# A hybrid decoder block in f32: how much fill each attention step is given

## The chip, the cores and the metric

The kernel runs on one core of a Trainium2 chip. The metric is device time in microseconds (us) of one execution, as the median of several. A core has five engines that run side by side and wait for each other through semaphores: TensorE (PE, matmuls; PEld its weight loads), VectorE (DVE), ScalarE (ACT), GpSimd (POOL) and SyncE (SP, which issues most DMAs). [...]

## The reference

One layer, 1024 tokens behind 16 meta tokens, model width 1024:

```python
h = rmsnorm(x, norm_g)
proj = jnp.einsum('bld,dn->bln', h, w_in)
u_pool, z_pool, q, k, v, z_attn, f_logit, g_pool, g_attn = jnp.split(proj, _split_points(), axis=-1)
y_pool = causal_multiscale_pool(u_pool, pool_w, pool_scale) * jax.nn.silu(z_pool)
log_f = jax.nn.log_sigmoid((f_logit + b_forget).astype(jnp.float32))
y_attn = forgetting_attention(q, k, v, log_f).reshape(B, L, ATTN_WIDTH) * jax.nn.silu(z_attn)
merged = (jax.nn.sigmoid(g_pool) * jnp.einsum('blc,cd->bld', y_pool, w_up_pool)
          + jax.nn.sigmoid(g_attn) * jnp.einsum('blc,cd->bld', y_attn, w_up_attn))
return x + jnp.einsum('bld,de->ble', merged, w_out)
```

The attention has 8 heads of width 64. The logit of query t and key s is q.k/8 plus the sum of the log forget gates between s and t, masked to be causal; then softmax and the product with v. A final rmsnorm follows and the meta tokens are dropped.

## The kernel before

**Precision.** Each f32 operand is split into a high part and a remainder, and a product is made of three matmuls (high x high, high x low, low x high), or two for the attention's score and value products, which carry both parts in one operand. The splits are work of ACT, DVE and POOL.

**Stages.** First the normalised input is transposed and q, k and v of the first pair of heads are projected. Then comes the attention, to about 460 us of the span. Then the gate projections (L973), the two up-projections (L170) and the output projection (L1232).

**The attention** works on 16 units: 4 pairs of heads, 2 heads of a pair, 2 halves of 512 queries. Keys come in blocks of 128 (`KB`). A unit of the first half has five key blocks, one of the second half nine. On the causal edge blocks get narrower: the widths are 512, 400, 272, 144, 16 for the first half, and four times 512 ahead of the same five for the second; these last five touch the diagonal.

- A *score step* (`qk`) makes two matmuls into a PSUM bank `ps` (L678, L679; two such banks), adds the gate term and, on the diagonal, the mask while copying the scores out (L685 DVE, L687 ACT), and updates a running maximum (L690 for the first block, L692 for the others).
- `maxes` finishes the maximum over the keys: two transposes, a reduction and two small maxima on DVE with small ACT copies between them, up to L710, which writes the maximum for all partitions.
- A *softmax step* (`soft`) subtracts the maximum (L719 DVE), takes the exponential (L720 ACT), splits the result in a high part (L723 ACT) and a remainder (L724 DVE), adds the block to the row sums (L730, L732 POOL), and makes the value product of the block two before it (`av`, L740: two matmuls into `po`). The remainder and high part have three buffers each (`NPH`), `LAG` is 2. The value products of a unit's last two blocks follow after all its steps.
- `finish` reads `po` out and stores it and the row sums.

In the loop over the units (L799 on) turn i lays the score steps of unit i+1 among the softmax steps of unit i (`merged`): both lists are spread evenly by width. So an even turn has the scores of a nine-block unit among the softmax of a five-block unit, and an odd one the other way round.

**The fill.** Between the steps PE is given other matmuls, the *fill*: the projections of q, k and v for the next pair of heads (with due times) and, freely, the projections of the pooling input and of the two gates (`f_u`, `f_raw`), which are evacuated by ACT and spilled to DRAM by SP. `Fill.pull(ns)` takes fill, matmul by matmul, until its booked price `mm_ns` (0.4219 ns a column, at least 107 ns) has used up ns; what was overdrawn is carried on as debt. What is left when the units are through is run by `F.drain()`. Who gets how much is written out in four places:

- each step of `merged` gets max(0, `PACE` x (DVE's time by a formula) - (PE's own time in the step)); the formulas stand in `a_steps` (scores) and `c_steps` (softmax);
- each of a unit's last two value products gets `LATENCY` ahead of it;
- `maxes` gets `LM1` = 1400 and `LM2` = 3200 (the first unit 2200 more);
- the gate computation ahead of the units gets ten times `LATENCY` in three pulls.

**The order.** PE's instructions run in the order of the program, which is written out by hand. Those of the other engines, in the attention, are ordered by the compiler's scheduler from their dependencies, priorities and its own expectation of when they can start. Once ordered, each engine takes its instructions strictly in that order. `after(x, y)` puts x behind y on their engine; `put` orders a transfer behind the last spill issued before it, `stores[-1]`.

In turn 13 the first weights of the gate stage are loaded (`g_raw0`), and in turn 14 ACT splits them (L821).

Of the kernel before, what the change touches and what calls it, by code (L numbers as in the profile page):

```python
# [22 lines left out]
KB = 128  # L23
# [7 lines left out]
PADS = {"lead": 32, "rest": 0}  # L31
HALVES = ((0, 512), (512, 1024))
PJ, PT = 3, 2
PACE = 1.67
LATENCY = 1800.0
LAT2 = 1600.0
LM1, LM2 = 1400.0, 3200.0
FIRST = 2200.0
NPH = 3
LAG = 2  # L40
# [5 lines left out]
def r32(ap):  # L46
    return ap.bitcast(F32)


def mm_ns(n):  # L50
    return max(n * 0.4219, 107.0)
# [3 lines left out]
def tile_hybrid_block(ctx, tc, x, meta, norm_g, w_in, b_forget, pool_w, pool_scale,  # L55
# [56 lines left out]
    def after(ins, prev):  # L112
        tc.add_manual_dep(ins.ins, prev.ins.name,
                          mybir.DependencyInfo(mybir.DependencyClass.NoSync, mybir.DependencyReason.DATA),
                          reason="order")
# [284 lines left out]
    F = Fill()  # L400
# [181 lines left out]
    def rows_of(t):  # L582
        return t.rearrange("(k p) c -> p k c", p=128)

    def put(dst, src):
        after(nc.sync.dma_start(dst, src), stores[-1])
# [56 lines left out]
    class Unit:  # L643
# [9 lines left out]
        def a_steps(self):  # L653
            for b in range(self.nb):
                w = 512 - self.c0[b]
                yield w, 1.04 * w + 70, 2 * mm_ns(w), (lambda b=b: self.qk(b))

        def c_steps(self):
            for b in range(self.nb):
                w = 512 - self.c0[b]  # L660
                yield w, 1.75 * w + 130, 2 * mm_ns(w), (lambda b=b: self.soft(b))

        def qk(self, b):
            p, e, q0, t0, kb, c0 = self.p, self.e, self.q0, self.t0, self.kb[b], self.c0[b]
# [95 lines left out]
    def merged(a, c):  # L760
        out_ = []
        for lst in (a, c):
            tot = sum(s[0] for s in lst) or 1
            acc = 0.0
            for s in lst:
                out_.append(((acc + 0.5 * s[0]) / tot, s))
                acc += s[0]
        for _, (w, dve, pe, f) in sorted(out_, key=lambda t: t[0]):
            f()
            F.pull(max(0.0, PACE * dve - pe))  # L770

# [8 lines left out]
    def pair_fill(p):  # L780
        if p < 4:
            F.add(f"q{p}", f_q(p))
            F.add(f"k{p}", f_k(p))
            F.add(f"v{p}", f_v(p), 4 * p - 2)
            F.add(f"v{p}", v_blocks(p, (6, 9), (0, 1)), 4 * p - 2, apart=True)
# [4 lines left out]
    def sums_at(i, tr):  # L790
        trs.append(tr)
        sums_of(i)
        if i % 4 == 1 and i > 1:
            add_y(i // 4 - 1)

    units = [Unit(p, e, half) for p in range(4) for e in range(2) for half in range(2)]
    merged(list(units[0].a_steps()), [])
    units[0].maxes(FIRST)
    for i, u in enumerate(units):  # L799
        nxt = units[i + 1] if i + 1 < 16 else None  # L800
        F.now = i
        if nxt is not None and nxt.p != u.p:
            F.until(f"q{nxt.p}", f"k{nxt.p}")
        merged(list(nxt.a_steps()) if nxt else [], list(u.c_steps()))
        for b in range(u.nb - LAG, u.nb):
            F.pull(LATENCY)
            u.av(b)
        if i == 1:
            after(nc.scalar.activation(pwh, pw, AF.Copy), exps[-1])
            nc.gpsimd.tensor_tensor(pwl, pw, r32(pwh), op=ALU.subtract)  # L810
        if nxt is not None:
            nxt.maxes(hook=lambda tr: sums_at(i, tr))
        u.finish()
        if i == 13:
            g_raw0 = [gp.tile([128, 2, 512], F32, name="graw", tag="g") for _ in range(2)]
            for k in range(2):
                put(g_raw0[k], rows_of(GSRC[0])[:, 2 * k:2 * k + 2])
        if i == 14:
            g_w0 = [[gp.tile([128, 2, 512], F32R, name="gw0", tag="g") for _ in range(2)] for _ in range(2)]
            for k in range(2):  # L820
                after(nc.scalar.activation(g_w0[0][k], g_raw0[k], AF.Copy), exps[-1])  # L821
                for c in range(0, 2):
                    for h0 in (0, 256):
                        after(nc.gpsimd.tensor_tensor(g_w0[1][k][:, c, h0:h0 + 256], g_raw0[k][:, c, h0:h0 + 256],
                                                      r32(g_w0[0][k][:, c, h0:h0 + 256]), op=ALU.subtract), accs[-1])
        if nxt is not None and nxt.p != u.p:
            F.until(f"v{nxt.p}")
            pair_fill(nxt.p + 1)
# [523 lines left out]
```

## Time and profile before

| | us |
|---|---|
| median of 3 runs | 727.25 (726.98 to 727.72) |
| the profiled execution's own time | 727.18 |
| its span, first to last instruction | 725.5 |

The profile is one execution. Its page gives the busy time of each engine; the view of stages gives the same for stretches of the span; the timeline has a row for each run of equal instructions: start, length, engine, line, operation, tiles, shape, count, and in brackets the idle time of the engine before it and what ended that. The end of a matmul is modelled and lies beyond the start of the next one in a back-to-back stream, so the time a matmul takes in a stream is read from start to start.

### The profile page before, as it was taken

How to read it: one execution, taken by the hardware profiler on the slowest of the kernel's cores; microseconds unless marked ns; L12 is line 12 of the kernel's file. 1: busy time of each engine (PE TensorE's matmuls, PEld its weight loads, DVE VectorE, ACT ScalarE, POOL GpSimd, SP SyncE). 2: the span in 40 equal slices, each digit the busy share in tenths (PEclk: the TensorE clock that was granted, in tenths of full speed). 3: DMA queues.
4: the chain of work that ended last, by engine and by line, in shares of the span. 5: the costliest groups of instructions: out<-in, count | busy, mean ns of one | idle time of the engine just before them, and what ended most of it. 6: DMA issues, size and time to landing. Idle time of an engine off the chain costs nothing.

```text
span 725.5 us, 10804 instructions
## 1 busy us (share of the span) xinstructions
PE 712.8 (98%) x3637; PEld 613.8 (85%) x3637; DVE 506.9 (70%) x913; ACT 422.4 (58%) x930; POOL 330.8 (46%) x409
## 2 busy tenths in 40 slices
PE   8999999999999999999999999999999999999996
PEld 6997999998888898898888878888888888888885
DVE  5753577667688676886768658765877545888775
ACT  6652577557686677676765576252776423525445
POOL 5412236639446584463653666493843010006152
PEclk9999999999999999999999999999999999999998
DMA  9201124782984868838576599486906267761006
GB/s 307 63 26 34 29 84 166 175 262 60 295 201 95 222 173 221 218 90 222 104 202 148 156 265 248 126 301 202 293 12 238 93 219 248 248 245 59 0 2 232
DMA packets 88506, 119.40 MB, mean 165 GB/s; under 512 B 11297, under 2 KB 54305, under 8 KB 86450
## 3 DMA queue, kind: packets, MB, share of 16 engines
q1 hardware_dynamic: 84896, 99.83, 43.0%
q0 software_dynamic: 2256, 16.25, 12.4%
q10 hardware_dynamic: 1298, 2.63, 1.0%
q8 instruction: 28, 0.46, 0.3%
q14 instruction: 28, 0.23, 0.1%
HBM read 92.81 MB, written 53.67 MB: 202 GB/s over the span
## 4 chain that ended last, share of the span: by engine, by line
PE 84%; ACT 3%; DVE 2%; DMA 1%; POOL 1%; issue 1%; POOLq 0%; ACTq 0%; DVEq 0%
PE pj L170 53%; PE pj L1232 8%; PE pj L973 8%; PE po L740 5%; PE pt L973 3%; PE pt L1232 2%; PE ps L679 2%; PE ps L678 2%; PE pj L515 1%; DMA graw<-in_w_in_dram 1%; POOL acc L732 1%; ACT S L687 1%; DMA raw<-in_w_in_dram 1%; ACT S L720 1%; PE pj L300 0%
## 5 line engine op out<-in xcount | busy, mean ns | idle before, releaser
L170 PE MATMUL pj<-hh,whi 128*128 128x512 f32 (+3 forms) x640 | 144.9, 352 | 0.0
L170 PE MATMUL pj<-hh,wlo 128*128 128x512 f32 (+3 forms) x640 | 143.2, 350 | 0.3 <-POOL wlo L434 0.3
L170 PE MATMUL pj<-hl,whi 128*128 128x512 f32 (+3 forms) x640 | 141.9, 350 | 0.0
L158 POOL TENSOR_TENSOR wlo<-raw,whi 128x256 fp32r<-128x256 f32 x116 | 90.7, 826 | 84.4 <-ACT whi L156 33.1
L170 PEld LDWEIGHTS pj<-hh,whi 128*128 128x128 f32 x640 | 108.0, 188 | 12.1 <-ACT hh L223 0.5
L170 PEld LDWEIGHTS pj<-hl,whi 128*128 128x128 f32 x640 | 108.1, 188 | 12.0
L170 PEld LDWEIGHTS pj<-hh,wlo 128*128 128x128 f32 x640 | 108.0, 188 | 12.0 <-POOL wlo L434 0.5
L724 DVE TENSOR_TENSOR pl<-S,ph 128x512 fp32r<-128x512 f32 (+4 forms) x112 | 83.5, 756 | 26.6 <-ACT ph L723 25.7
L732 POOL TENSOR_TENSOR acc<-acc,S 128x272 f32<-128x272 f32 (+4 forms) x80 | 74.4, 930 | 14.5 <-ACT S L720 9.3
L692 DVE TENSOR_TENSOR pt<-pt,S 128x400 f32<-128x400 f32 (+2 forms) x96 | 46.8, 487 | 44.7 <-ACT S L687 43.1
L687 ACT ACTIVATE S<-ps,negc 128x400 f32<-128x400 f32 (+2 forms) x96 | 48.5, 514 | 37.0 <-DVE S L685 33.0
L136 POOL TENSOR_TENSOR gw<-graw,gw 128x256 fp32r<-128x256 f32 x40 | 45.5, 1173 | 29.8 <-ACT gw L953 12.2
L723 ACT ACTIVATE ph<-S 128x512 fp32r<-128x512 f32 (+4 forms) x112 | 52.7, 479 | 9.6 <-PE po L740 9.2
L720 ACT ACTIVATE S<-S 128x512 f32<-128x512 f32 (+4 forms) x112 | 49.8, 478 | 13.3 <-DVE S L719 13.2
L719 DVE TENSOR_TENSOR S<-S,pt 128x512 f32<-128x512 f32 (+4 forms) x112 | 50.7, 498 | 0.6
L1125 DVE TENSOR_TENSOR rl<-pj,rl 128x512 f32<-128x512 f32 x32 | 22.0, 690 | 28.7 <-PE pj L170 28.4
L973 PE MATMUL pj<-gh,gw 128*128 128x512 f32 x180 | 42.0, 389 | 0.0
L156 ACT ACTIVATE whi<-raw 128x512 fp32r<-128x512 f32 x58 | 33.8, 622 | 11.6 <-DMA raw<-in_w_in_dram 5.1
L973 PEld LDWEIGHTS pj<-gh,gw 128*128 128x128 f32 x180 | 33.8, 188 | 7.1
L678 PE MATMUL ps<-qa,ka 128*128 128x512 f32 (+4 forms) x112 | 36.5, 326 | 3.2 <-ACT S L687 3.2
L679 PE MATMUL ps<-ql,ka 128*128 128x512 f32 (+4 forms) x112 | 37.5, 335 | 0.0
L740 PE MATMUL po<-pl,V 128*128 128x512 f32 (+4 forms) x112 | 37.4, 334 | 0.0
(229 smaller groups left out, 1304.7 us busy)
## 6 DMA issues: line engine op xcount, KB each, us to landing
raw<-in_w_in_dram SPq DMA_DIRECT2D x31, 512.0 KB, 5.2
gs<-in_w_in_dram SPq DMA_DIRECT2D x5, 1024.0 KB, 9.9
td<-in_w_out_dram SPq DMA_DIRECT2D x5, 1024.0 KB, 8.4
xt<-in_x_dram SPq DMA_DIRECT2D x8, 512.0 KB, 7.4
sp_gp<-st SPq DMA_DIRECT2D x16, 256.0 KB, 4.6
gs<-gs POOLq DMA_DIRECT2D x4, 1024.0 KB, 9.1
td<-td POOLq DMA_DIRECT2D x4, 1024.0 KB, 11.3
sp_ga<-st SPq DMA_DIRECT2D x16, 256.0 KB, 4.4
```

The lines of the kernel that those rows point to most:

```text
L158: ins = nc.gpsimd.tensor_tensor(lo[:, k:k + 2], raw[:, k:k + 2], r32(hi[:, k:k + 2]), op=ALU.subtract)
L170: nc.tensor.matmul(ps, a, b, start=(i == 0), stop=(i == len(seq) - 1))
L678: nc.tensor.matmul(ps[:kb, c0:], ka[:, k0:k0 + kb], qa[:, q0 + c0:q0 + 512], start=True, stop=False)
L679: nc.tensor.matmul(ps[:kb, c0:], ka[:, k0:k0 + kb], ql[:, q0 + c0:q0 + 512], start=False, stop=True)
L687: nc.scalar.activation(s[:kb, f0:], ps[:kb, f0:], AF.Identity, bias=nb_)
L720: exps.append(nc.scalar.activation(s[:kb, c0:], s[:kb, c0:], AF.Exp))
L723: nc.scalar.activation(ph[:kb, c0:], s[:kb, c0:], AF.Copy)
L724: dves.append(nc.vector.tensor_tensor(pl[:kb, c0:], s[:kb, c0:], r32(ph[:kb, c0:]), op=ALU.subtract))
L732: accs.append(nc.gpsimd.tensor_tensor(acc[:kb, c0:], acc[:kb, c0:], s[:kb, c0:], op=ALU.add))
L740: nc.tensor.matmul(self.po[:, c0:], v, r[:kb, c0:], start=(b == 0 and i == 0), stop=(b == self.nb - 1 and i == 1))
L973: nc.tensor.matmul(ps, op_w[n][p][k // 2][:, k % 2, i * 128:(i + 1) * 128], op_h[n][q][k // 2][:, k % 2], start=start and m == 0, stop=m = ...
L1232: nc.tensor.matmul(ps, pick(A_, k, p)[:, i * 128:(i + 1) * 128], pick(B_, k, q)[:, c0:c1], start=start and n == 0, stop=n == 11, skip_grou ...
```

## The change

Five numbers in the planner's formulas change, and a new constant is used ahead of a unit's last two value products. `LATENCY` itself and its use in the gate computation stay.

```diff
-PACE = 1.67
+PACE = 1.1
 LATENCY = 1800.0
 LAT2 = 1600.0
 LM1, LM2 = 1400.0, 3200.0
+TAIL = 900.0
...
         def a_steps(self):
             for b in range(self.nb):
                 w = 512 - self.c0[b]
-                yield w, 1.04 * w + 70, 2 * mm_ns(w), (lambda b=b: self.qk(b))
+                yield w, 1.05 * w + 165 + 300 * (b * KB + KB > self.t0), 2 * mm_ns(w), (lambda b=b: self.qk(b))
...
         def c_steps(self):
             for b in range(self.nb):
                 w = 512 - self.c0[b]
-                yield w, 1.75 * w + 130, 2 * mm_ns(w), (lambda b=b: self.soft(b))
+                yield w, 2.6 * w + 376, 2 * mm_ns(w), (lambda b=b: self.soft(b))
...
         for b in range(u.nb - LAG, u.nb):
-            F.pull(LATENCY)
+            F.pull(TAIL)
             u.av(b)
```

The added 300 stands for a block that touches the diagonal. No instruction, transfer or buffer is added or taken away: the same fill matmuls stand at other places between the same steps.

## The prediction

> **What bounds the kernel now.** I read the head of the page first.
>
> ```profile
> span 725.5 us, 10804 instructions
> PE 712.8 (98%) x3637; PEld 613.8 (85%) x3637; DVE 506.9 (70%) x913; ACT 422.4 (58%) x930; POOL 330.8 (46%) x409
> ```
>
> TensorE (PE) is busy 98% of the span, VectorE (DVE) 70%. The view of stages shows whether the attention, where the change acts, differs from the stages behind it (columns: length, busy time and count of PE, weight loads, DVE, ACT, POOL, granted clock).
>
> ```profile
> 375.43:398.24 22.81, 22.81 (x108) 19.04 (x107) 16.61 (x32) 14.96 (x35) 10.36 (x15) 1.00 0.71 184
> ...
> 421.36:444.50 23.14, 21.84 (x103) 17.94 (x102) 14.75 (x32) 15.02 (x33) 12.85 (x18) 1.00 0.94 267
> ...
> 555.36:642.40 87.04, 87.04 (x385) 72.10 (x385) 56.02 (x82) 36.99 (x50) 5.76 (x8) 1.00 0.66 226
> ```
>
> The first row is one interval of the attention (one turn of the unit loop): PE is never idle, DVE is busy 73% of it. The second, the last with scores in it, has 1.3 us of idle PE. The third is a stage without any stall. From the chain of work that ended last:
>
> ```profile
> 460.61 12.82 PE pj L170 x56
> ...
> 555.36 87.04 PE pj L170 x384
> ```
>
> In the stall-free stage a 512-column matmul takes 87.04/384 = 0.227 us; the planner books 0.4219 x 512 = 216 ns, so planned fill costs 1.05 times its booked price. The first row is fill that was still left when the last value product was done (12.8 us, run by `F.drain`). Waits of PE in the attention:
>
> ```profile
> PE ps L678 <- ACT S L687: 3.2, 6, 1.3
> ```
>
> All six are one kind: a score matmul waits until ScalarE (ACT) has copied an older score out of one of the two `ps` banks. No value product waits for DVE. The modelled end of a matmul lies after the next one's start, so a stall is longer than its idle time. The timeline of PE gives it from starts:
>
> ```profile
> 84.61 0.66 PE L170 MATMUL pj<-hh,whi 128*128 128x272 f32 x4
> 85.43 0.39 PE L678 MATMUL ps<-qa,ka 128*128 128x272 f32 x1 [0.15 <-ACT S L687]
> ...
> 85.79 0.67 PE L170 MATMUL pj<-hl,whi 128*128 128x272 f32 x4
> 86.69 0.34 PE L678 MATMUL ps<-qa,ka 128*128 128x144 f32 x1 [0.23 <-ACT S L687]
> ...
> 145.79 0.70 PE L170 MATMUL pj<-hh,whi 128*128 128x384 f32 x3
> 147.17 0.50 PE L678 MATMUL ps<-qa,ka 128*128 128x512 f32 x1 [0.69 <-ACT S L687]
> ...
> 200.15 0.63 PE L170 MATMUL pj<-hh,whi 128*128 128x512 f32 x2
> 201.33 0.33 PE L678 MATMUL ps<-qa,ka 128*128 128x144 f32 x1 [0.55 <-ACT S L687]
> ...
> 332.70 0.63 PE L170 MATMUL pj<-hh,wlo 128*128 128x512 f32 x2
> 333.63 0.50 PE L678 MATMUL ps<-qa,ka 128*128 128x512 f32 x1 [0.30 <-ACT S L687]
> ...
> 427.06 1.07 PE L170 MATMUL pj<-hh,whi 128*128 128x512 f32 x4
> 429.42 0.51 PE L678 MATMUL ps<-qa,ka 128*128 128x512 f32 x1 [1.29 <-ACT S L687]
> ```
>
> Start to start, less the run between at 0.227 us a matmul (by width 0.170 for 384 columns and 0.120 for 272), the stalls are 0.34 + 0.42, 0.87, 0.73, 0.48 and 1.45: **4.3 us in all**, 0.6% of the run. The rest of the attention is PE work of fixed length. Fill that is moved does not shorten it: the change can win at most these 4.3 us, and loses by making new stalls.
>
> **The change, part by part.** *What the planner gives out.* A score step of width w got max(0, 1.67(1.04w+70) - 2mm), and gets 1.1(1.05w+165) - 2mm, with 300 more inside the bracket for a block on the diagonal. For 512 columns: 574 to 341 ns, on the diagonal 671. For 400, 272, 144 and 16 columns (always diagonal): 474 to 636, 360 to 596, 153 to 464, 0 to 316. Softmax steps: 1281 to 1446, 1049 to 1220, 783 to 962, 424 to 611, 50 to 245. The two tails: 3600 to 1800 a unit. Summed with the unchanged 4600 of `maxes`: an interval that lays the scores of a nine-block unit among the softmax of a five-block one goes from 15644 to 14931 ns; one with a nine-block softmax from 18473 to 19351; the first scores alone from 1561 to 2683; the last unit from 12312 to 12068. Over 16 units: 268.3 to 269.7 us. So 1.4 us less fill is left for the end, about 11.4 of the 12.8: PE does not run dry, and the stages behind start at the same amount of PE work. No instruction, transfer or wait is added; only PE's order changes, and with it when ACT, DVE, POOL and SP get their evacuations, weight splits and spills.
>
> *More at softmax steps: worth nothing.* The tightest value product that I found:
>
> ```profile
> 225.79 0.75 DVE L724 TENSOR_TENSOR pl<-S,ph 128x272 fp32r<-128x272 f32 x1
> ...
> 226.60 0.37 PE L740 MATMUL po<-ph,V 128*128 128x272 f32 x1
> 226.81 0.29 PE L740 MATMUL po<-pl,V 128*128 128x272 f32 x1
> ```
>
> DVE was done at 226.54, PE came at 226.81: 0.27 us of slack, and no wait. More fill widens that; there was nothing to win. DVE was not late for softmax anywhere.
>
> *Less at the tails, and less at full-width score steps.* Both bring PE sooner to the waits for score copies. Take the last score of a five-block unit (16 columns), the end of its maximum (L710, from which the next softmax starts), and the first and fourth score matmul of the nine-block unit that follows:
>
> ```profile
> 328.51 0.40 PE L678 MATMUL ps<-qa,ka 128*128 128x512 f32 x1
> ...
> 365.78 0.17 PE L678 MATMUL ps<-qa,ka 128*128 128x16 f32 x1
> ...
> 375.43 0.40 PE L678 MATMUL ps<-qa,ka 128*128 128x512 f32 x1
> ...
> 380.06 0.39 PE L678 MATMUL ps<-qa,ka 128*128 128x512 f32 x1
> ...
> 411.74 0.17 PE L678 MATMUL ps<-qa,ka 128*128 128x16 f32 x1
> ```
> ```profile
> 325.79 0.73 DVE L710 STREAM_TRANSPOSE pt<-mz 128x512 f32<-128x512 f32 x1
> ...
> 370.76 0.73 DVE L710 STREAM_TRANSPOSE pt<-mz 128x512 f32<-128x512 f32 x1
> ...
> 416.24 0.73 DVE L710 STREAM_TRANSPOSE pt<-mz 128x512 f32<-128x512 f32 x1
> ```
>
> Last score to next unit's first: 9.65 us on PE. Booked in between: 0+50+3600+4600 = 8250 before, 316+245+1800+4600 = 6961 after, so 1289 x 1.05 = 1.35 less: 8.30. The maximum ends 5.71 (371.49 - 365.78) or, where DVE was prompt, 5.23 us (416.97 - 411.74) after that last score. The longer steps ahead of it let DVE catch up, so I take 5.2 to 5.5. PE then reaches the first score 2.8 to 3.1 us after the maximum, where it was 375.43 - 371.49 = 3.94. First to fourth score: 4.63 before; four steps in between change by -233+165-233-233 = -534 ns, so 4.07. The fourth score comes 6.9 to 7.2 us after the maximum; before it came 8.57.
>
> Its bank is free when ACT has copied the second score. ACT runs the softmax exponentials first (L720, from 372.24 on), then weight splits and copies:
>
> ```profile
> 331.87 1.14 ACT L156 ACTIVATE whi<-raw 128x512 fp32r<-128x512 f32 x2
> 332.91 1.25 ACT L687 ACTIVATE S<-ps,negc 128x512 f32<-128x512 f32 x2
> ...
> 372.24 0.63 ACT L720 ACTIVATE S<-S 128x512 f32<-128x512 f32 x1 [0.92 <-DVE S L719]
> ...
> 375.59 1.14 ACT L156 ACTIVATE whi<-raw 128x512 fp32r<-128x512 f32 x2
> 376.63 0.67 ACT L687 ACTIVATE S<-ps,negc 128x512 f32<-128x512 f32 x1
> 377.33 0.60 ACT L690 ACTIVATE pt<-S 128x512 f32<-128x512 f32 x1
> 377.87 0.58 ACT L342 ACTIVATE st<-pj 128x512 f32<-128x512 f32 x1
> 378.66 0.69 ACT L687 ACTIVATE S<-ps,negc 128x512 f32<-128x512 f32 x1 [0.20 <-PE ps L679]
> ```
>
> In the second group ACT waited only 0.20 us, so without PE the copy could end at 379.15, 7.66 us after the maximum. In the first it released PE at 333.63, 7.11 after 326.52 (and PE, at 328.51 only 1.99 us behind that maximum, stalled). So ACT needs 7.1 to 7.7 us and PE will allow 6.9 to 7.2: a stall of 0 to 0.8 us, middle 0.4, in each of the seven intervals of this kind behind the first. **2.8 us (0 to 5.6)**. Before, three of these seven stalled behind the full-width scores and one at a 144-column score (0.87, 0.48, 1.45, 0.73: 3.5).
>
> *More at narrow score steps.* In front of 85.43 PE gets 97+162 = 259 ns more (x1.05 = 0.27 of the 0.34), in front of 86.69 another 236 (0.25 of 0.42). The copies there are ordered by ACT's queue; I book a gain of 0.4 of the 0.76. The stall at 201.33 sits behind two score steps that together get 585 ns more, and goes.
>
> *The last interval.* Its stall has a cause of its own:
>
> ```profile
> 427.73 1.06 ACT L821 ACTIVATE gw<-graw 128x1024 fp32r<-128x1024 f32 x1 [2.52 <-DMA graw<-in_w_in_dram]
> ```
>
> A score copy lies behind this on ACT. The transfer is issued behind a spill (`put` comes after `stores[-1]`). At that point 2.4 us more fill is done than before (1122 + 7 x (878 - 713) ns, times 1.05), so the spill and the transfer can come up to 2.4 us earlier against PE's scores. I leave 0.5 us of it beyond the ordinary stall, bounds 0 and 1.5.
>
> Sum after: 0.3 (first unit) + 2.8 + 0.5 + 0.3 for stalls like that at 201.33 at new places (bounds 0 and 1, one seen in 15 intervals) = 3.9, against 4.3. The profiled execution took 727.18 us (its span 725.5), 0.07 under the median 727.25; **forecast 727.18 - 0.4 = 726.8**: no change that can be told.
>
> [...]
>
> **The rivals.** *Slower: the score run meets ACT's softmax burst.* Same mechanism as above at its bad end. ACT keeps its order, with weight splits ahead of the second copy (7.7 us), and PE allows 6.9: 7 x 0.8 = 5.6, the last transfer as before (1.5), first unit 0.3, others 1.0: 8.4, or 4.1 more: **731.3**. It decides from a mean stall of 0.6 us a long-score interval on (7 x 0.6 + 0.3 + 0.5 + 0.6 = 5.6, 1.3 over now). For it: two intervals with a lead near 2 us stall today (147.17, 333.63). Against: leads will be 2.8 to 3.1. Chance 0.25.
>
> *Faster: the copies move up.* Only PE's order is written out; the compiler orders ACT by when it expects things ready. If, with scores due sooner, it puts their copies between the exponentials, the second ends under 6.9 us and the seven stalls go: 0.3 + 0.3 + 0.3 left, 3.4 won: **723.8**. For it: exponentials have slack. Against: nothing shows the compiler's view. Chance 0.25.
>
> *The edit does nothing:* total fill differs by 0.5%, softmax was not late, and the stalls are set by ACT's queue wherever PE stands. Then only the first unit's 0.4 goes: 726.8, inside the forecast; its chance is in it.
>
> [...] Chance 0.02, as the stall-free row speaks against it.
>
> **How the numbers follow.** About 0.2% (1.45 us) is what a measurement of this kernel tells from no change. Forecast (within 1.45) 0.48, slower 0.25, faster 0.25 + 0.02. The range takes in most of both rivals: 724.2 to 730.6.
>
> **What would show it.** Right: PE waits remain `ps L678 <- ACT S L687`, now small ones at third and fourth scores of many nine-block units rather than a few large; none at 201 or for L740; the final run of fill near 11.4 us; first score about 3 us behind L710. Wrong: leads under 2.5 us or over 4, waits of L740 for DVE, ACT copying scores between exponentials, or a stall over 1 us at a new place.

## The result, and the profile after

| | us | ratio to before (95%) |
|---|---|---|
| before, 4 runs | 727.12 (726.64 to 727.72) | |
| after, 4 runs | 733.65 (732.87 to 734.59) | 1.009 [1.0073, 1.0107] |
| the profiled execution of after | 732.87, its span 731.2 | |

The change makes the kernel 6.5 us slower; the forecast was 726.8, the range 724.2 to 730.6. From profile to profile the span grew by 731.2 - 725.5 = 5.7 us, and those are what the trace can explain. Lines 38 and up of before are one higher in after (L687 is L688, L821 is L822).

The head of the page of after:

```profile
span 731.2 us, 10818 instructions
PE 713.9 (98%) x3637; PEld 615.6 (84%) x3637; DVE 509.7 (70%) x913; ACT 424.2 (58%) x930; POOL 334.2 (46%) x409
```

PE's count is the same and its busy time 1.1 us more. The waits of PE in the attention (total, times, longest):

```profile
PE ps L679 <- ACT S L688: 7.4, 5, 5.2
...
PE pj L171 <- DVE V L311: 0.8, 1, 0.8
```

The kind is the one of before, but one of the five waits is 5.2 us long. PE's timeline, around it and at the other waits:

```profile
147.47 0.50 PE L679 MATMUL ps<-qa,ka 128*128 128x512 f32 x1 [0.99 <-ACT S L688]
...
241.22 0.50 PE L679 MATMUL ps<-qa,ka 128*128 128x512 f32 x1 [0.70 <-ACT S L688]
...
262.56 0.70 PE L171 MATMUL pj<-hh,whi 128*128 128x512 f32 x2 [0.79 <-DVE V L311]
...
335.60 0.50 PE L679 MATMUL ps<-qa,ka 128*128 128x512 f32 x1 [0.33 <-ACT S L688]
...
424.24 0.39 PE L679 MATMUL ps<-qa,ka 128*128 128x512 f32 x1
...
427.72 0.63 PE L171 MATMUL pj<-hh,whi 128*128 128x512 f32 x2
433.53 0.79 PE L679 MATMUL ps<-qa,ka 128*128 128x512 f32 x1 [5.18 <-ACT S L688]
434.12 0.63 PE L680 MATMUL ps<-ql,ka 128*128 128x512 f32 x1
434.55 1.48 PE L171 MATMUL pj<-hh,whi 128*128 128x512 f32 x3
435.83 1.35 PE L171 MATMUL pj<-hl,whi 128*128 128x512 f32 x4
437.02 0.40 PE L679 MATMUL ps<-qa,ka 128*128 128x512 f32 x1
```

Start to start as in the prediction, the long stall is 433.53 - 427.72 - 2 x 0.227 = 5.36 us. It stands in the interval where before had 1.45: 3.9 more. Then nine matmuls take 437.02 - 433.53 = 3.49 us where 2.04 are due: 1.4 more. The view of stages says why (columns as in the prediction; the clock is the third from the end), and the chain that ended last has the stall-free stage:

```profile
429.57:432.98 3.41, 0.00 (x0) 0.00 (x0) 0.00 (x0) 1.62 (x3) 0.91 (x3) 1.00 1.08 353
432.98:436.39 3.41, 2.86 (x7) 2.28 (x8) 2.10 (x3) 2.60 (x4) 3.41 (x6) 0.50 0.94 286
```
```profile
561.04 87.04 PE pj L171 x384
```

The clock was at half, 0.50, from 432.98 to 436.39, so the first matmuls behind the stall took nearly twice their time (three from 434.55 to 435.83: 0.43 us each). The stall-free stage is as long as before, 87.04 us. So **5.3 us are one event in the last interval with scores**: 3.9 of waiting and 1.4 of slow clock. The other stalls sum to 4.05 us (0.27 in the first unit, 0.32 at the first nine-block scores, 1.15, 0.87, 0.95, 0.49), against 2.84 before without the 1.45: 1.2 more. The attention itself began earlier in this execution (its first score at 82.6 us, 83.2 before): 5.3 + 1.2 - 0.6 = 5.9, of the 5.7 that the span shows.

What ACT did there (timeline of ACT, after):

```profile
425.52 0.67 ACT L688 ACTIVATE S<-ps,negc 128x512 f32<-128x512 f32 x1
426.22 0.60 ACT L691 ACTIVATE pt<-S 128x512 f32<-128x512 f32 x1
...
431.36 1.06 ACT L822 ACTIVATE gw<-graw 128x1024 fp32r<-128x1024 f32 x1 [4.54 <-DMA graw<-in_w_in_dram]
...
432.80 1.26 ACT L688 ACTIVATE S<-ps,negc 128x512 f32<-128x512 f32 x2
```

ACT copies the first score, then comes to the split of the first gate weights (L822) and sits idle for 4.54 us until they land. The copy of the second score, which frees the bank that PE needs for its fourth, stands behind it in ACT's order. In before the split stood one copy later, behind this one (ACT, before):

```profile
424.52 0.69 ACT L687 ACTIVATE S<-ps,negc 128x512 f32<-128x512 f32 x1 [0.36 <-PE ps L679]
```

And the landing. SP's queue and POOL's, after; then the same two of before:

```profile
421.75 0.32 SPq L344 DMA_DIRECT2D sp_ga<-st  x1
...
422.70 1.06 SPq L587 DMA_DIRECT2D graw<-in_w_in_dram  x2
```
```profile
417.69 0.81 POOL L591 DMA_DIRECT2D td<-td  x1 [5.28 <-DVE mt L698]
418.25 1.07 POOL L617 DMA_DIRECT2D sp_y<-sp_y  x1
```
```profile
421.64 1.04 SPq L586 DMA_DIRECT2D graw<-in_w_in_dram  x2
```
```profile
413.62 0.81 POOL L590 DMA_DIRECT2D td<-td  x1 [3.85 <-DVE mt L697]
```

The weights were issued at 422.70 and landed at 431.36, 8.66 us later; before, 421.64 and 427.73, 6.09. They are tied to a spill of the fill (`stores[-1]`), the accumulating transfer to the unit's maximum (`mt`). Tails are shorter now, so the spill came earlier against the maximum, and the weights left 5.0 us behind the accumulation where it had been 8.0. A second, smaller one (`sp_y`) starts right behind it. What the two take there, from the view of DMAs of after for 410 to 440 us (times, KB each, us from issue to landing):

```profile
td<-td POOLq DMA_DIRECT2D x1, 1024.0 KB, 8.0
...
sp_y<-sp_y POOLq DMA_DIRECT2D x1, 512.0 KB, 11.1
```

So when the weights left, `td` was in flight for another 417.69 + 8.0 - 422.70 = 3.0 us and `sp_y` for 6.7. In before the two take 8.7 and 11.3 us, and it was 0.7 and 3.9.

### The profile page after: what moved, and what is told of

It is laid out like the page before. It is cut to its first block, busy times and chain, and to the rows that moved or that the text cites. A ratio compares the mean times of both kernels' runs of the same rounds, so it can differ in the third digit from the quotient of the medians.

```text
span 731.2 us, 10818 instructions
## 1 busy us (share of the span) xinstructions
PE 713.9 (98%) x3637; PEld 615.6 (84%) x3637; DVE 509.7 (70%) x913; ACT 424.2 (58%) x930; POOL 334.2 (46%) x409
## 3 DMA queue, kind: packets, MB, share of 16 engines
q0 software_dynamic: 2256, 16.25, 12.6%
## 4 chain that ended last, share of the span: by engine, by line
PE 83%; ACT 5%; DVE 3%; issue 1%; DMA 1%; POOLq 0%; POOL 0%; ACTq 0%; DVEq 0%; SPq 0%
PE pj L171 52%; PE pj L1233 8%; PE pj L974 8%; PE po L741 5%; PE pt L974 3%; PE pt L1233 2%; PE ps L680 2%; PE ps L679 2%; DMA graw<-in_w_in_dram 1%; PE pj L516 1%; ACT S L721 1%; ACT S L688 1%; ACT ph L724 1%; DVE pl L725 1%; ACT whi L157 1%
## 5 line engine op out<-in xcount | busy, mean ns | idle before, releaser
L171 PE MATMUL pj<-hh,whi 128*128 128x512 f32 (+3 forms) x640 | 146.9, 355 | 0.8 <-DVE V L311 0.8
L171 PE MATMUL pj<-hl,whi 128*128 128x512 f32 (+3 forms) x640 | 144.0, 351 | 0.0
L688 ACT ACTIVATE S<-ps,negc 128x400 f32<-128x400 f32 (+2 forms) x96 | 48.7, 516 | 46.0 <-DVE S L686 41.3
L137 POOL TENSOR_TENSOR gw<-graw,gw 128x256 fp32r<-128x256 f32 x40 | 48.1, 1236 | 28.2 <-ACT gw L954 12.8
## 6 DMA issues: line engine op xcount, KB each, us to landing
td<-in_w_out_dram SPq DMA_DIRECT2D x5, 1024.0 KB, 11.3
```

What stands on the lines that cost most here:

```text
L171: nc.tensor.matmul(ps, a, b, start=(i == 0), stop=(i == len(seq) - 1))
L688: nc.scalar.activation(s[:kb, f0:], ps[:kb, f0:], AF.Identity, bias=nb_)
```

## The experiments

Two theories stood first. **A**: the event above is the loss; the weights, tied to the fill, meet the accumulation and block ACT one copy earlier. **B**, the slower rival of the prediction: scores come too soon behind the maximum in all turns, and the last one is only the worst of many.

**1. Away with the blocked split.** The split of the weights goes one turn later, in after and in before.

```diff
-        if i == 14:
+        if i == 15:
             g_w0 = [[gp.tile([128, 2, 512], F32R, name="gw0", tag="g") for _ in range(2)] for _ in range(2)]
```

> The changed kernel with the split of the first gate weights (ACT, L822) moved from turn 14 to turn 15, so that no score copy stands behind it on ACT. Theory A (one transfer): of the 6.5 us lost, 5.3 are the stall of 5.35 us at the fourth score of the last nine-block unit (1.45 before) and the 1.4 us at a lower clock behind it. Then this takes 726.5 to 728.5 us, with at most an ordinary stall of 0 to 0.8 us left at that place and a granted clock of 1.00 throughout the attention. Theory B (spread): the lost time is the price of sooner scores in all turns, and a stall removed here comes back elsewhere: 731 us or more.

> The kernel before with the same move. Theory A: the stall of 1.45 us in the last turn goes, 725.6 to 726.3 us; so the two distributions of fill differ by about 1 us without the transfer. Theory B: no change from 727.1, as the fill was balanced, and 4 us or more between this and the changed kernel with the move.

`after_split15`: 728.15 (725.66 to 730.89, 12 runs), 1.0017 [1.0003, 1.0031]. The stall at 427.9 and the slow clock are gone (the mean granted clock of the profiled execution is 0.997; after had 0.994) and nearly all of the loss with them, as A has it. New stalls of 1.0 to 1.2 us stand in the gate stage, where the split now is. `before_split15`: 733.56 (733.2 to 734.79, 4 runs), 1.0097 [1.0084, 1.011]. Here the expectation missed. The 1.45 us stall went, but PE then stalled 4.86 us at 478.7, in the gate stage, and the mean granted clock of this execution was 0.994 (0.997 in before). ACT's timeline of it:

```profile
482.22 1.06 ACT L953 ACTIVATE gw<-graw 128x1024 fp32r<-128x1024 f32 x1 [6.20 <-DMA sp_y<-t]
483.19 0.58 ACT L342 ACTIVATE st<-pj 128x512 f32<-128x512 f32 x1
```

It is the same trap at another place: a later split of gate weights waits on ACT for a transfer, and the copy that frees PE's bank stands behind it. So a move of a few microseconds in what SP and ACT do costs as much as the change itself, at another place.

**2. The weights earlier.** The load moves one turn up, with after's numbers and with before's.

```diff
-        if i == 13:
+        if i == 12:
             g_raw0 = [gp.tile([128, 2, 512], F32, name="graw", tag="g") for _ in range(2)]
```

> The changed kernel with the load of the first gate weights put out one turn sooner (turn 12), the split left in turn 14. Theory A: the transfer has landed when ACT comes to the split, ACT loses only the 2.1 us of the two splits there, and the stall falls from 5.35 us to between 0 and 2: 727 to 729.5 us. Theory B: 731 us or more.

> The kernel before with the load of the first gate weights in turn 12, as the control to the same move in the changed kernel (727.72). Theory A (one transfer): its stall of 1.45 us in the last turn with scores goes or becomes an ordinary one: 725.5 to 726.7 us, so that the distributions of fill as such differ by 1 to 2 us. Theory B (spread): no gain, 726.7 or more.

`after_load12`: 727.72 (727.36 to 728.37, 11 runs), 1.0014 [1.0005, 1.0023]. `before_load12`: 725.76 (725.18 to 726.73, 11 runs), 0.9989 [0.998, 0.9997]. In the first the weights were there (ACT, `after_load12`):

```profile
425.06 1.04 ACT L822 ACTIVATE gw<-graw 128x1024 fp32r<-128x1024 f32 x1
```

There is no wait in brackets, the stall there falls from 5.36 to 1.49, and the mean granted clock is 0.999. **B falls as the main cause**: with the event out of the way some 5.5 of the 6.5 us are back (1.0014 against 1.009). The two kernels tell what the new numbers cost without it, and that is what is left for B: 727.72 - 725.76 = 2.0 us, with intervals that don't touch. Their stalls in the attention sum to 5.42 and 3.55, 1.9 apart.

**3. The accumulating transfer out of the way.** Theory A's second half: is the late landing due to the accumulation? `td` goes one turn later.

```diff
-        13: [(add, TD[2], TD[3])],
-        14: [(add, GS[4], GS[2]), (add, TD[4], TD[2])],
+        14: [(add, TD[2], TD[3]), (add, GS[4], GS[2]), (add, TD[4], TD[2])],
```

> The changed kernel with one accumulating transfer of 1 MB (td, issued 5.0 us ahead of the gate weights at 417.69) moved from turn 13 to turn 14. If the weights took 8.66 us to land (6.09 before) because they share the DMA engines with it, they land 1.5 to 2.5 us sooner, and the stall falls by as much, perhaps below the point where the clock drops: 729.5 to 732 us. If only the place of the split on ACT counts, nothing changes: 733.6 us.

732.06 (729.11 to 734.48, 4 runs), 1.0071 [1.0047, 1.0095]. The weights came sooner than expected, and the time gained less than that. SP, the smaller accumulation in the view of DMAs, and ACT (the split is L821 here):

```profile
422.55 1.09 SPq L587 DMA_DIRECT2D graw<-in_w_in_dram  x2
```
```profile
sp_y<-sp_y POOLq DMA_DIRECT2D x1, 512.0 KB, 5.2
```
```profile
427.05 1.06 ACT L821 ACTIVATE gw<-graw 128x1024 fp32r<-128x1024 f32 x1 [0.49 <-DMA graw<-in_w_in_dram]
...
462.66 0.60 ACT L343 ACTIVATE st<-pj 128x512 f32<-128x512 f32 x1 [8.64 <-DMA sp_ga<-st]
```

Issued at the same time, the weights land in 4.50 us rather than 8.66, and the stall is 1.32: the accumulation in flight is what made them late. With `td` away the smaller one takes 5.2 us instead of 11.1 and is gone too when the weights leave, so how much each of the two held them up is not told apart. But `td` is now under way one turn later, where a spill lands late; in the profiled execution PE stalls 3.79 us at 459.6 behind the copy in the last row. The gain was given back 32 us later, more in some runs than in others.

**4. The parts alone**, on before. The other two keep `PACE` at 1.67 and so scale the new formula by 1.1/1.67.

```diff
-            F.pull(LATENCY)
+            F.pull(TAIL)
```
```diff
-                yield w, 1.04 * w + 70, 2 * mm_ns(w), (lambda b=b: self.qk(b))
+                yield w, (1.1 / PACE) * (1.05 * w + 165 + 300 * (b * KB + KB > self.t0)), 2 * mm_ns(w), (lambda b=b: self.qk(b))
```
```diff
-                yield w, 1.75 * w + 130, 2 * mm_ns(w), (lambda b=b: self.soft(b))
+                yield w, (1.1 / PACE) * (2.6 * w + 376), 2 * mm_ns(w), (lambda b=b: self.soft(b))
```

> The kernel before with the shorter tails alone (900 for 1800 ns, twice a unit). PE then comes to the next scores 1.9 us sooner after every unit, and the accumulating transfers that start with the maximum are 1.9 us less ahead of the gate weights. Theory A: this part brings the big stall in turn 14, 3 us or more there, and the time is 730 to 734 us. Theory B: stalls of 0.5 us and more at the fourth scores in all turns, and the time is 730 us or more with no stall over 2 us.

> The kernel before with the new formula of the score steps alone. From first to fourth score PE is 0.73 us sooner; the lead ahead of the first is 0.3 us longer. Theory A: fourth scores stall by up to 0.5 us more each where ACT is dense, the stall in turn 14 by 0.5 us more: 727 to 729 us. Theory B: most of the 6.5 us comes from here: 730 us or more.

> The kernel before with the new formula of the softmax steps alone. No value product waited for DVE before, so under both theories nothing is won: 726.5 to 728 us; the fill that is left at the end shrinks by some 19 us to nothing, so the last unit may run out of fill and wait for DVE at the value products, which would add 1 to 3 us.

| | median us | ratio to before (95%) |
|---|---|---|
| `tail_only` | 733.05 (732.09 to 735.75, 4 runs) | 1.0094 [1.0076, 1.0111] |
| `score_only` | 737.67 (736.53 to 739.78, 4 runs) | 1.0155 [1.014, 1.017] |
| `soft_only` | 736.8 (735.92 to 738.0, 4 runs) | 1.0138 [1.0122, 1.0153] |

Each part alone costs 6 to 11 us and the three together 6.5: they do not add. `tail_only` came as theory A expected; the sizes of the other two missed. The profiles show two reasons. First, the tails and the softmax formula shift where the weights fall. ACT in `tail_only` and in `soft_only`:

```profile
408.43 1.06 ACT L822 ACTIVATE gw<-graw 128x1024 fp32r<-128x1024 f32 x1 [5.50 <-DMA graw<-in_w_in_dram]
```
```profile
445.67 1.06 ACT L821 ACTIVATE gw<-graw 128x1024 fp32r<-128x1024 f32 x1 [4.65 <-DMA graw<-in_w_in_dram]
```

PE stalls there by 4.34 and 3.20 us. Second, the two that give out more fill leave hardly any for the end (1.7 us in `score_only`, none in `soft_only`), and the gate stage starts before its inputs are ready. PE's waits in `score_only`:

```profile
PE ps L678 <- ACT S L687: 4.9, 6, 2.4
PE pt L973 <- DVE zp L988: 2.7, 1, 2.7
PE pj L973 <- POOL gw L136: 2.1, 2, 1.2
```

The two rows of L973 are the gate stage. Start to start, PE lost 7.7 us there, 4.8 of them in these waits; the mean granted clock of this execution was 0.993 (6.5 us were lost in `soft_only`, which lost another 3.2 at its last value products, with no fill left between them; 0.3 in after). The 2.4 us in the first row are of another kind: ACT waited for DVE's last softmax step ahead of the score copy, where PE's lead behind the maximum was only 1.94 us. The change as a whole keeps its fill for the end only because its three parts nearly cancel: 11.24 us of it are left there, where `tail_only` has 42.95.

**5. One tail put back**, to send the weights later with everything else as in after.

```diff
-            F.pull(TAIL)
+            F.pull(LATENCY if i == 13 else TAIL)
```

> The changed kernel with the old 1800 ns ahead of the last two value products of unit 13 alone, the unit ahead of the turn with the big stall; the other fifteen keep 900. PE then comes 1.9 us later, against the maximum and the transfers, to the scores of the last unit. Theory A (one transfer in one turn): the stall of 5.35 us falls to about 3.4 and most of the clock's loss of 1.4 us may go with it: 729.5 to 732 us, from 1.8 us of fill in 270. Theory B (spread): one tail of sixteen is worth 0.4 us, 733 us or more.

732.86 (732.09 to 733.75, 4 runs), 1.0079 [1.0062, 1.0096]. The number missed. The 1800 ns more of fill passed the next spill, so that the weights were tied to that one (SP and ACT):

```profile
430.11 0.53 SPq L344 DMA_DIRECT2D sp_ga<-st  x1
430.74 0.97 SPq L587 DMA_DIRECT2D graw<-in_w_in_dram  x2
```
```profile
437.00 1.06 ACT L822 ACTIVATE gw<-graw 128x1024 fp32r<-128x1024 f32 x1 [5.74 <-DMA graw<-in_w_in_dram]
```

They left 8 us later and held up the copy of the fifth score instead; PE stalled by 4.76 us at the seventh, which needs that bank. The place of this transfer moves in steps of a whole spill.

**6. The other way.** If the lead of the first score behind the maximum decides about the ordinary stalls, more lead than before should be faster. These start from `before_load12`. In odd turns, which end with the maximum ahead of the nine-block scores, the tails get 400 or 800 ns more each, and the 512-wide steps 135 or 270 less, so that the total stays.

```diff
-    def merged(a, c):
+    def merged(a, c, cut=0.0):
...
-            F.pull(max(0.0, PACE * dve - pe))
+            F.pull(max(0.0, PACE * dve - pe - cut * (w == 512)))
...
-        merged(list(nxt.a_steps()) if nxt else [], list(u.c_steps()))
+        merged(list(nxt.a_steps()) if nxt else [], list(u.c_steps()), 135.0 if i % 2 and nxt else 0.0)
...
-            F.pull(LATENCY)
+            F.pull(LATENCY + 400.0 * (i % 2 and nxt is not None))
```

> The opposite of the change, on the kernel before with the load in turn 12 (725.76): in odd turns (a five-block unit's scores) 400 ns more ahead of each of the last two value products and 135 ns less at each of the six full-width steps, so that the total stays and PE comes 0.84 us later to the nine-block scores. If the small stalls are set by PE's lead against ACT's burst of exponentials, those at 145, 331 and 424 (0.84, 0.46, 0.66 us) shrink: 724.3 to 725.3 us. If ACT's order sets them wherever PE stands: 725.8 +- 0.5.

> The same with 800 ns more ahead of each of the two and 270 ns less at each of the six steps: PE comes 1.68 us later. By the lead, the stalls at 145, 331 and 424 are gone: 723.8 to 724.8 us, unless value products now wait for DVE in odd turns (slack 0.3 us at the least before the change) or the gate stage starts too soon. By ACT's order alone: 725.8 +- 0.7.

`lead400`: **723.63** (723.18 to 725.33, 5 runs), 0.9958 [0.9944, 0.9971]: faster than before, after and `before_load12`. `lead800`: 724.69 (724.54 to 725.59, 7 runs), 0.9972 [0.9961, 0.9983]. PE's waits in each:

```profile
PE ps L678 <- ACT S L687: 0.9, 3, 0.5
```
```profile
PE po L740 <- DVE pl L724: 0.7, 1, 0.7
```

In `lead400` the first score of the interval at 372.93 follows the maximum by 5.08 us (3.95 in `before_load12`), the stalls at 145, 331 and 424 us are gone, and the span is 2.0 us shorter. `lead800` has the same stalls gone, but a value product waits for DVE: a stall of 0.99 us at 315.6. Its doubled shift brings nothing more.

## Why the prediction was wrong, step by step

- *The bound and what can be won* (PE's fixed work, stalls of 4.3 us): right. In `lead400`, the load's move included, stalls of 1.4 us are left (0.32, 0.40, 0.72), 2.9 fewer, and the median is 0.42% or 3.1 us lower; 0.8 of its 4.0 us shorter span lie ahead of the attention (first score at 82.43 us).
- *What the planner gives out*: right. The final run of fill on the chain of waits of after:

```profile
467.91 11.24 PE pj L171 x49
```

  11.24 us were forecast as about 11.4.
- *More at softmax worth nothing*: right as far as after goes; no value product waits for DVE in it. I took the cost to be nothing too, and alone it is 10 us (`soft_only`), by way of the fill at the end and the weights.
- *Less at tails and score steps*: PE's own path was right, the lead only in part. Turn 12 of after in the timelines of PE, of DVE (its maximum) and of ACT (a score copy ahead of an exponential):

```profile
369.83 0.17 PE L679 MATMUL ps<-qa,ka 128*128 128x16 f32 x1
...
378.08 0.39 PE L679 MATMUL ps<-qa,ka 128*128 128x512 f32 x1
...
381.99 0.39 PE L679 MATMUL ps<-qa,ka 128*128 128x512 f32 x1
```
```profile
374.06 0.73 DVE L711 STREAM_TRANSPOSE pt<-mz 128x512 f32<-128x512 f32 x1
```
```profile
379.10 0.67 ACT L688 ACTIVATE S<-ps,negc 128x512 f32<-128x512 f32 x1
379.67 0.32 ACT L721 ACTIVATE S<-S 128x144 f32<-128x144 f32 x1
```

  Last score to first score is 8.25 us (forecast 8.30; 8.2 to 8.4 in all six such intervals ahead of the last), first to fourth 3.91 (4.07), the lead 378.08 - 374.79 = 3.29. I had read the lead from one interval and forecast 2.8 to 3.1 for all. In the order of the intervals it was 2.47, 3.28, 2.50, 2.80, 2.56 and 3.30, and the three below 2.6 are the three that stalled, by 1.15, 0.87 and 0.49. "Many small ones" was wrong: half of the intervals have none. The mean, 0.42 each where I took 0.4, is partly luck, as ACT's order did not stay as I had taken it either (see the rivals).
- *Narrow score steps*: the first unit kept 0.27 of its 0.76, where I left 0.3. The stall at 201 is gone, as forecast. The 0.3 us for new places was 0.95, one wait for DVE's V at 261.5.
- **The last interval: this step failed.** I wrote that the transfer "can come up to 2.4 us earlier against PE's scores" and priced it at 0.5, bounds 0 and 1.5. The issue did come earlier: 1.54 us ahead of the first score, where it had been 0.28 behind it. The landing went the other way, to 7.12 us behind the first score from 6.37: the sum had no term for the transfer's own time, which grew from 6.09 to 8.66 us, and I did not look at what else would be in flight. Nor did I ask where ACT's order would put the split: one copy earlier it holds up the fourth score (3.9 us behind the first) rather than the fifth (6.6). And I had no term for the clock. Measured: a stall of 5.36 us, and 1.4 of slow clock behind it: 6.8 where the forecast had the ordinary 0.4 and 0.5 on top. All the bounds of the sum came from small waits; the row with a DMA as its releaser was in the prediction, but the bound put on it was no more than the stall that it already made.
- *The rivals*: the slower one named 731.3, near the time that came, but by a mechanism that did not happen (mean stall 0.42, not 0.8). The faster one happened in part, though the time did not show it: in four of the six intervals ahead of the last, turn 12 among them, the copy of the first score now stands ahead of the last two exponentials, where in before it stood behind them all. Three of these four have no stall.

Shown: that the blocked split makes nearly all of the loss (`after_split15`, `after_load12`), that the accumulation makes the landing late (`after_td14`, 4.50 against 8.66 us), that lead pays (`lead400`). Left open: why the compiler put the split one copy earlier in after, which was not tried by itself, and why `after_split15` and `after_td14` differ by 5 us from run to run.

## What to carry to other kernels

When work is moved on the bound engine, list every transfer whose issue is tied to that work and every in-order engine that waits for it, and price each by what else will be in flight and by all that is queued behind the wait; here that was worth more than all the steps whose durations were worked out. An instruction that waits for a transfer must not stand ahead of PSUM copies on an in-order engine (in after ACT sat idle for 4.54 us with the copy behind it, and PE stalled 5.36 us): load it a turn earlier, as `before_load12` does. Change one interval's share with the total held constant, since what is given out is missing where a later stage needs cover.

## What the runs showed of the hardware

**The clock was at half behind some stalls and not behind others.** In after it was 0.50 for 3.41 us, from 432.98 on, behind the stall of 5.36 us; in before the last interval with scores, with its stall of 1.45 us, had 1.00. The same view in `score_only`, around its wait of 2.4 us, and in `tail_only`:

```profile
337.80:342.00 4.20, 1.62 (x6) 0.67 (x4) 1.75 (x3) 2.28 (x5) 3.59 (x6) 1.00 0.54 129
342.00:345.80 3.80, 3.43 (x9) 2.68 (x10) 2.10 (x3) 1.58 (x3) 0.00 (x0) 0.59 0.53 173
```
```profile
225.30:229.20 3.90, 1.58 (x6) 0.67 (x4) 3.19 (x6) 3.88 (x11) 3.90 (x6) 0.99 1.04 205
229.20:232.40 3.20, 3.16 (x8) 2.50 (x9) 2.10 (x3) 1.85 (x3) 2.74 (x5) 0.50 0.76 202
```

PE was idle for 2.6 and 2.3 us of the first rows, and the clock of the second rows was 0.59 and 0.50 in the mean. PE in `soft_only`, at the last value products:

```profile
476.31 0.39 PE L740 MATMUL po<-ph,V 128*128 128x272 f32 x1 [2.68 <-ACT ph L723]
...
477.38 1.18 PE L973 MATMUL pj<-hh,gw 128*128 128x512 f32 x4
478.40 1.09 PE L973 MATMUL pj<-hl,gw 128*128 128x512 f32 x4
479.33 2.02 PE L973 MATMUL pj<-hh,gw 128*128 128x512 f32 x8
481.19 1.09 PE L973 MATMUL pj<-hl,gw 128*128 128x512 f32 x4
```

Here the wait is 2.7 us, longer than the one in `score_only`. Start to start the four matmuls from 477.38 took 0.26 us each and those from 478.40 0.23, against 0.43 behind the stall of after: no half clock is seen there. So the length of a single wait did not tell whether the slow clock would come on top; what decides it was not shown.

**The first of a pair of 512 KB loads took 4.5 to 10.6 us to land**: 4.50 in `after_td14`, 6.09 in before, 8.66 in after, 10.6 in `tail_only`. That an accumulating transfer in flight makes it slow is shown by `after_td14` against after. The rest of the spread may have other causes: in `after_tail13` the loads left 13.2 and 12.6 us behind the two accumulations, which in after took 8.0 and 11.1, and the first of them took 6.26.
